# Module boundaries of a hybrid conformer and DeltaNet trunk: scaled activations in two PSUM banks, three tiles begun, weight subtractions on VectorE

## The chip, the cores and the metric

The kernel runs on one core of a Trainium2 chip (trn2). The time is device microseconds of one execution of the whole program. A core has five engines, each with its own queue of instructions: PE (TensorE, matmuls), DVE (VectorE), ACT (ScalarE), POOL (GpSimd) and SP (SyncE, which here issues the loads). They meet by semaphores. SBUF is the core's working memory; PSUM is the memory that matmuls write to, in eight banks of 512 float32 columns on 128 partitions.

## What is computed

A decoder trunk of two layers on 512 tokens of 1024 channels, batch 1. Each layer is a SwiGLU feed-forward module (FFN), a mixer, and a second FFN; the mixer is a causal convolution module in layer 0 and a gated DeltaNet in layer 1. Every module's input is normalised and modulated, and its output is added to the trunk through a gate:

```python
mod = (cs @ w_ada[i] + b_ada[i]).reshape(B, N_SUB, 3, D)
def modulated(x, j):
    shift, scale = mod[:, j, 0][:, None, :], mod[:, j, 1][:, None, :]
    return rms_norm(x, norm_g[i, j]) * (1.0 + scale) + shift
def gate(j):
    return 1.0 + mod[:, j, 2][:, None, :]
h = modulated(x, 0)
x = x + FFN_RES_WEIGHT * gate(0) * swiglu_ffn(h, w_ffn_in[i, 0], w_ffn_out[i, 0])
h = modulated(x, 1)
x = x + gate(1) * y          # y: conv_module(h) or gated_deltanet(h)
h = modulated(x, 2)
x = x + FFN_RES_WEIGHT * gate(2) * swiglu_ffn(h, w_ffn_in[i, 1], w_ffn_out[i, 1])
return rms_norm(x, final_g)  # after the last layer
```

## The kernel before

The trunk `x` lies in SBUF with channels on partitions, as eight blocks of 128 channels (k = 0 to 7) by 512 tokens. Float32 products are made of three matmuls: each operand is split into a high half, rounded to the matmul's type, and a low half, the remainder, and `mm3` adds high × high, low × high and high × low (L173, L174, L175) into one PSUM bank. A weight block comes by DMA as `raw`; ACT casts it to `whi` and DVE (L164, L165) or, at the boundaries, POOL (L206, L207) subtracts to get `wlo`. Activations likewise have `hh` and `hl`. Four buffers hold split weights, three hold raw ones.

In the FFNs `Feed` loads and splits weights ahead of the block that uses them: `block` prepares one more (`prep`) and takes the oldest ready one (`take`). In the FFNs of the first layer DVE also computes the modulation, by row sums `ajunk` over `w_ada` (L417), a few for each block (`ada_step`), with the rest in `ada_drain` ahead of `tail`.

Inside a module PE is fed densely. Where one module ends and the next begins stands `tail` (L210), at six places. It makes the last two blocks of output channels (6 and 7) in two halves of 256 tokens. For each half come the residual on DVE (`res`, L236), the square on ACT (L392), the sum over blocks on DVE (`ssum`, L397), the sum over channels on PE (`root`, L373, written to `aux`), the square root on ACT (L244), the reciprocal on DVE (L250) and the spread of the result over all partitions on PE (`bcast`, L368). Then `run` goes through k: `scaled` makes `t` on DVE (L260) and `hh` on ACT (L262), `low` makes `hl` on DVE (L272), and `head_k` issues the matmuls of the next module's first tiles. How many tiles are begun is in `EN`, by (layer, module). While half 0 runs, hooks at chosen k (`EH`) place half 1's residual, accumulation, root and spread, and one more weight split on POOL.

The region runs under a fixed order, so each engine executes as written here. Where only two tiles are begun, the third is made by 512-wide matmuls, of which some are filled in behind the second half's k. For `t` there are two buffers in SBUF. The last tail normalises for the output and has no next module.

The five that begin a module are, by time: FFN to convolution (near 390 us), convolution to FFN (600), FFN to the next layer's FFN (970), FFN to DeltaNet (1340), DeltaNet to FFN (1730).

Of the kernel before, what the change touches and what calls it, by code (L numbers as in the profile page):

```python
# [15 lines left out]
P = 128  # L16
T = 512
H2 = T // 2
D = 1024
KT = D // P  # L20
# [22 lines left out]
ENG={mybir.EngineType.PE,mybir.EngineType.Activation,mybir.EngineType.DVE,mybir.EngineType.Pool,mybir.EngineType.SP}  # L43
# [5 lines left out]
ARB = 3  # L49
# [10 lines left out]
ER = 7  # L60
EH = [1,2,3,3,5,6]
FH = [3,4,5,6]
MPL = [(),()]
EN = {(0,1):2,(0,2):2,(1,0):2,(1,1):3,(1,2):2}
LOP = [4,5,17,18,19,20,21,22,23,24]
IW = 3
IQ = [2,2,3,3]
# [40 lines left out]
def trunk_kernel(ctx: ExitStack, tc: tile.TileContext, x_in, c_in, vecs, consts, w_ada, w_st,  # L108
                 w_fi, w_fo, w_glu, w_tz, w_pw, w_dn, w_do, out):
    nc = tc.nc  # L110
    pe, act, dve, pool = nc.tensor, nc.scalar, nc.vector, nc.gpsimd

    keep = ctx.enter_context(tc.tile_pool(name="keep", bufs=1))
    wp = ctx.enter_context(tc.tile_pool(name="wp", bufs=4))
# [15 lines left out]
    def scratch(tag, shape=(P, T), dt=F32, bufs=1):  # L130
        return sc.tile(list(shape), dt, tag=tag, name=nm(tag), bufs=bufs)
# [22 lines left out]
    def load_raw(src, nk):  # L154
        raw = wp.tile([P, KT, P], F32, tag="raw", name=nm("raw"), bufs=3)
        with tc.high_priority(offset=WPRI):
            nc.sync.dma_start(raw[:, :nk, :], src)
        return raw

    def split_w(raw, nk):  # L160
        whi = wp.tile([P, KT, P], F32R, tag="whi", name=nm("whi"))
        wlo = wp.tile([P, KT, P], F32R, tag="wlo", name=nm("wlo"))
        with tc.high_priority(offset=WPRI):
            act.copy(whi[:, :nk, :], raw[:, :nk, :])  # L164
            dve.tensor_tensor(wlo[:, :nk, :], raw[:, :nk, :], whi[:, :nk, :].bitcast(F32), ALU.subtract)  # L165
        return whi, wlo

    def load_w(src, nk):
        return split_w(load_raw(src, nk), nk)
# [30 lines left out]

    edge = {}

    def split_pool(raw):
        whi = wp.tile([P, KT, P], F32R, tag="whi", name=nm("whi"))
        wlo = wp.tile([P, KT, P], F32R, tag="wlo", name=nm("wlo"))
        act.copy(whi, raw)  # L206
        pool.tensor_tensor(wlo, raw, whi.bitcast(F32), ALU.subtract)  # L207
        return whi, wlo

    def tail(src, nkt, mhi, mlo, layer, sub, norm, nxt, feed=None):  # L210
        nlayer, nsub, srcs = nxt or (0, 0, [])
        ms = (KT - 2, KT - 1)
        ps = {(m, i): mm_tile()[:, :H2] for m in ms for i in range(2)}
        if feed:
            feed.prep()
            ws = {m: feed.take() for m in ms}
            hw = feed.ready + [split_w(*r) for r in feed.raws]
        else:
            ws = {m: load_w(src(m, 0, KT), KT) for m in ms}
            hw = [load_w(s, KT) for s in srcs[:2]]  # L220
        raws = [load_raw(s, KT) for s in srcs[2:]]
        preload(AF.Sqrt, x[:, KT - 3, :1])
        region = ExitStack()
        region.enter_context(tc.manual_schedule(engines=ENG))

        sts = {}

        def mms(m, i, ks):
            sl = halves[i]
            for k in ks:  # L230
                mm3(ps[m, i], ws[m], k, mhi[:, k, sl], mlo[:, k, sl], k == 0, k == KT - 1)

        def res(m, i):
            j = (layer * 3 + sub) * KT + m
            sl = halves[i]
            dve.scalar_tensor_tensor(x[:, m, sl], ps[m, i], gate[:, j:j + 1], x[:, m, sl], ALU.mult, ALU.add)  # L236
            sts["sq"] = norm.square(x[:, m, sl], sl)
            return sts["sq"]

        def root(i):  # L240
            st = sts[i]
            pt = aux_tile()
            col_sum(pt, norm.t[:, halves[i]], 0)
            act.activation(st, pt[:, :2], AF.Sqrt, bias=eps, scale=1.0 / D)  # L244

        for i in range(2):
            sts[i] = scratch("rst", (P, 2), bufs=2)

        def inv_root(i):
            dve.reciprocal(sts[i], sts[i])  # L250

        def bcast(i):
            return spread([sts[i][:, g:g + 1] for g in range(2)])

        tv, hv = {}, {}

        def scaled(pb, k, i):
            j = (nlayer * 3 + nsub) * KT + k
            tv[k] = t = scratch("t", bufs=2)[:, :H2]
            dve.scalar_tensor_tensor(t, x[:, k, halves[i]], gain[:, j:j + 1], pb[:, :H2], ALU.mult, ALU.mult)  # L260
            shift = mod[:, nlayer, nsub * 24 + k:nsub * 24 + k + 1]
            act.activation(hh[:, k, halves[i]], t, AF.Identity, bias=shift)  # L262
            if k in MPL[i]:
                hv[k] = scratch("sil", bufs=2)[:, :H2]
                act.activation(hv[k], t, AF.Identity, bias=shift)

        def low(k, i):
            sl = halves[i]
            if k in MPL[i]:
                pool.tensor_tensor(hl[:, k, sl], hv[k], hh[:, k, sl].bitcast(F32), ALU.subtract)  # L270
                return
            dve.scalar_tensor_tensor(hl[:, k, sl], tv[k], mod[:, nlayer, nsub * 24 + k:nsub * 24 + k + 1],  # L272
                                     hh[:, k, sl].bitcast(F32), ALU.add, ALU.subtract)

        def head_k(i, k):
            sl = halves[i]
            for m, p in enumerate(hp):
                w = hw[m] if m < 2 else more[m - 2]
                mm3(p[:, sl], w, k, hh[:, k, sl], hl[:, k, sl], k == 0, k == KT - 1)

        def run(i, pb, hooks):
            for k in range(KT):
                scaled(pb, k, i)
                if k:
                    low(k - 1, i)
                    head_k(i, k - 1)
                for f in hooks.get(k, ()):
                    f()
            low(KT - 1, i)
            head_k(i, KT - 1)  # L290

        def final(i, pb, hooks):
            sl = halves[i]
            for k in range(KT):
                hooks.get(k, lambda: None)()
                dve.scalar_tensor_tensor(x[:, k, sl], x[:, k, sl], V("final_g", k), pb[:, :H2], ALU.mult, ALU.mult)
                if k % 2:
                    (nc.scalar if i and k % 4 == 3 else nc.sync).dma_start(out[i, :, k - 1:k + 1, :], x[:, k - 1:k + 1, sl])

        every = range(KT)  # L300
        mms(ms[0], 0, every)
        sq = res(ms[0], 0)
        mms(ms[1], 0, every)
        norm.accum(sq, halves[0])
        sq = res(ms[1], 0)
        norm.accum(sq, halves[0])
        mms(ms[0], 1, range(ER))
        root(0)
        inv_root(0)
        mms(ms[0], 1, range(ER, KT))  # L310
        more = [split_pool(raws[0])] if raws else []
        sq = res(ms[0], 1)
        mms(ms[1], 1, range(EK))
        pb = bcast(0)
        mms(ms[1], 1, range(EK, KT))
        if nxt is None:
            norm.accum(sq, halves[1])
            final(0, pb, {FH[0]: lambda: res(ms[1], 1), FH[1]: lambda: norm.accum(sts["sq"], halves[1]),
                          FH[2]: lambda: root(1), FH[3]: lambda: inv_root(1)})
            final(1, bcast(1), {})  # L320
            region.close()
            return
        box = {}
        hp = [mm_tile() for _ in range(EN[nlayer, nsub])]

        def late_res():
            box["sq"] = res(ms[1], 1)

        def late_root():
            root(1)  # L330

        def late_bcast():
            box["pb"] = bcast(1)

        hooks = {0: [lambda: norm.accum(sq, halves[1])]}
        for k, f in zip(EH, (late_res, lambda: norm.accum(box["sq"], halves[1]),
                             lambda: more.append(split_pool(raws[1])), late_root, lambda: inv_root(1), late_bcast)):
            hooks.setdefault(k, []).append(f)
        run(0, pb, hooks)
        run(1, box["pb"], {})  # L340
        region.close()
        edge["ps"], edge["w"] = hp, hw + more
# [78 lines left out]

    def ada_step(n):
        for _ in range(n):
            if len(ada["fly"]) == ARB:
                ada_use()
            ada_load()

# [17 lines left out]
    ada = {"plan": [], "fly": []}  # L445
# [37 lines left out]
    def ffn(layer, which, nxt, first=None):  # L483
# [4 lines left out]
        with tc.tile_pool(name=nm("ffn"), bufs=1) as ap, ExitStack() as ax:  # L488
# [15 lines left out]
            region = ax.enter_context(ExitStack())  # L504
            region.enter_context(tc.manual_schedule(engines=ENG))
            box = {}

            def step(n):
                if pump:
# [1248 lines left out]
```

## Time and profile before

| what | value |
|---|---|
| runs of the kernel, us | 2110.41, 2110.07, 2097.76; median 2110.07 |
| profiled execution, us | 2109.84, of which the span of the trace is 2108.1 |
| mean granted clock of TensorE | 0.977 |
| busy time of PE, DVE, ACT, POOL, us | 2022.4, 1209.2, 769.5, 226.2 |
| weight subtractions on DVE (L165, 128x1024 and 128x896) | 296, 361.6 us in all |
| weight subtractions on POOL (L207) | 11, mean 2404 ns |
| `t` (L260), `hh` (L262), `hl` (L272), mean of 80 each, ns | 478, 507, 629 |

A row of the timeline has the start, the length, the engine, the line and operation, output and inputs by name, and in brackets how long the engine was idle just before and what ended that. A row of the windows view has the stretch, its length, the busy time and count of PE, weight loads, DVE, ACT and POOL, the granted clock (1.00 is full), the DMA engines' share and GB/s. A row of PE's waits has the total in us, how often, and the longest. The lines of these views that matter stand in the prediction.

### The profile page before, as it was taken

To read this page: it belongs to the slowest core of one execution; us is meant where nothing else is said; L and a number is where in the kernel's file an instruction comes from. 1 tells how busy PE (TensorE), PEld (TensorE's weight loads), DVE (VectorE), ACT (ScalarE), POOL (GpSimd) and SP (SyncE) were. 2 spreads that over 40 slices of the span, in tenths; PEclk is the share of its full clock that TensorE was granted. 3 is DMA by queue.
4 is the path that set the end of the run, shared out by engine and by line. 5 is a ranking of instruction groups with operands and counts; after the bars stand their busy time and mean duration, and the time that the engine had idled before them with its cause. 6 is when DMAs were issued, how large, how long until landed. Compare 5 with 4: busy or idle time off the path is not lost.

```text
span 2108.1 us, 26022 instructions
## 1 busy us (share of the span) xinstructions
PE 2022.4 (96%) x10258; PEld 1683.7 (80%) x10258; DVE 1209.2 (57%) x1819; ACT 769.5 (37%) x1316; POOL 226.2 (11%) x150
## 2 busy tenths in 40 slices
PE   6999999898899999999999999989899999999998
PEld 4888888787888888888888888877677788888887
DVE  7666666799865655536333333777945574333334
ACT  5422222375542222224222222565345643222222
POOL 0000000289200000000000000125310100000000
PEclk9999999899899999999999999999989999999999
DMA  7667766222235656432333333322211132333332
GB/s 279 213 223 234 228 230 229 95 80 90 60 111 187 202 196 210 154 100 80 87 104 97 95 99 92 112 74 64 64 57 31 41 120 79 92 99 92 98 100 70
DMA packets 78332, 262.04 MB, mean 124 GB/s; under 512 B 8321, under 2 KB 14081, under 8 KB 78082
## 3 DMA queue, kind: packets, MB, share of 16 engines
q1 hardware_dynamic: 77666, 259.87, 38.6%
q8 instruction: 80, 1.31, 0.3%
q10 hardware_dynamic: 544, 0.52, 0.1%
q14 instruction: 42, 0.34, 0.1%
HBM read 254.59 MB, written 5.77 MB: 124 GB/s over the span
## 4 chain that ended last, share of the span: by engine, by line
PE 84%; DVE 8%; POOL 3%; ACT 2%; issue 2%; DMA 0%; POOLq 0%; DVEq 0%; SPq 0%; ACTq 0%
PE mm L173 26%; PE mm L174 25%; PE mm L175 25%; POOL pacc L661 3%; DVE t L1090 1%; PE mm L1415 1%; DVE hl L272 1%; DVE x L1166 1%; DVE x L1161 1%; PE mm L1437 1%; PE mm L1423 1%; PE mm L1642 1%; PE mm L1643 1%; PE aux L368 1%; PE mm L1646 1%
## 5 line engine op out<-in xcount | busy, mean ns | idle before, releaser
L174 PE MATMUL mm<-hl,whi 128*128 128x512 f32 (+1 forms) x1944 | 737.3, 380 | 17.2 <-DVE hl L272 16.6
L173 PE MATMUL mm<-hh,whi 128*128 128x512 f32 (+1 forms) x1944 | 742.6, 384 | 1.8 <-ACT hh L884 1.8
L175 PE MATMUL mm<-hh,wlo 128*128 128x512 f32 (+1 forms) x1944 | 734.7, 379 | 1.8 <-DVE wlo L165 1.8
L165 DVE TENSOR_TENSOR wlo<-raw,whi 128x1024 fp32r<-128x1024 f32 (+1 forms) x296 | 361.6, 1223 | 305.2 <-ACT whi L164 303.5
L174 PEld LDWEIGHTS mm<-hl,whi 128*128 128x128 f32 x1944 | 371.1, 191 | 87.0 <-DVE hl L272 22.0
L175 PEld LDWEIGHTS mm<-hh,wlo 128*128 128x128 f32 x1944 | 370.9, 191 | 71.5 <-DVE wlo L165 2.6
L173 PEld LDWEIGHTS mm<-hh,whi 128*128 128x128 f32 x1944 | 370.0, 191 | 71.5 <-issue 4.8
L164 ACT CAST whi<-raw 128x1024 fp32r<-128x1024 f32 (+1 forms) x296 | 301.7, 1023 | 247.3 <-PE mm L174 228.0
L173 PE MATMUL mm<-ahi,whi 128*128 128x512 f32 (+1 forms) x768 | 289.7, 377 | 0.0
L175 PE MATMUL mm<-ahi,wlo 128*128 128x512 f32 (+1 forms) x768 | 287.5, 374 | 0.0
L174 PE MATMUL mm<-alo,whi 128*128 128x512 f32 (+1 forms) x768 | 285.2, 371 | 0.0
L530 ACT CAST ahi<-t 128x512 fp32r<-128x512 f32 x88 | 54.7, 622 | 378.7 <-DVE t L526 378.7
L175 PEld LDWEIGHTS mm<-ahi,wlo 128*128 128x128 f32 x768 | 145.1, 189 | 28.2
L174 PEld LDWEIGHTS mm<-alo,whi 128*128 128x128 f32 x768 | 145.2, 189 | 27.0
L522 ACT ACTIVATE sil<-mm 128x512 f32<-128x512 f32 x88 | 52.7, 598 | 307.5 <-PE mm L175 303.8
L173 PEld LDWEIGHTS mm<-ahi,whi 128*128 128x128 f32 x768 | 145.4, 189 | 24.2
L207 POOL TENSOR_TENSOR wlo<-raw,whi 128x1024 fp32r<-128x1024 f32 x11 | 26.4, 2404 | 1226.6 <-ACT whi L206 1226.6
L417 DVE CUSTOM_DVE_ANT_0 ajunk<-araw,cs 128x1024 bf16<-128x1024 f32 x128 | 156.1, 1220 | 0.7
L526 DVE TENSOR_TENSOR t<-sil,mm 128x512 f32<-128x512 f32 x88 | 60.5, 688 | 157.8 <-PE mm L175 148.3
L461 DVE SCALAR_TENSOR_TENSOR x<-mm,gate,x 128x512 f32<-128x512 f32 x64 | 48.1, 751 | 143.5 <-PE mm L175 143.5
L531 DVE TENSOR_TENSOR alo<-t,ahi 128x512 fp32r<-128x512 f32 x88 | 60.9, 693 | 60.8 <-ACT ahi L530 60.8
L661 POOL TENSOR_TENSOR pacc<-pacc,pr 128x492 f32<-128x492 f32 (+11 forms) x58 | 83.3, 1437 | 18.6 <-ACT pr L660 14.5
(259 smaller groups left out, 1719.5 us busy)
## 6 DMA issues: line engine op xcount, KB each, us to landing
raw<-in_w_fi_dram SPq DMA_DIRECT2D x169, 512.0 KB, 3.5
araw<-in_w_ada_dram SPq DMA_DIRECT2D x128, 512.0 KB, 4.5
raw<-in_w_fo_dram SPq DMA_DIRECT2D x64, 448.0 KB, 3.3
raw<-in_w_dn_dram SPq DMA_DIRECT2D x33, 512.0 KB, 3.6
raw<-in_w_fo_dram SPq DMA_DIRECT2D x32, 512.0 KB, 3.5
stage<-in_w_ada_dram SPq DMA_DIRECT2D x16, 512.0 KB, 6.3
raw<-in_w_glu_dram SPq DMA_DIRECT2D x16, 512.0 KB, 3.5
raw<-in_w_pw_dram SPq DMA_DIRECT2D x8, 512.0 KB, 3.7
```

Of the source, the lines that this page charges most:

```text
L164: act.copy(whi[:, :nk, :], raw[:, :nk, :])
L165: dve.tensor_tensor(wlo[:, :nk, :], raw[:, :nk, :], whi[:, :nk, :].bitcast(F32), ALU.subtract)
L173: pe.matmul(ps, whi[:, k, :], mhi, start=first, stop=False)
L174: pe.matmul(ps, whi[:, k, :], mlo, start=False, stop=False)
L175: pe.matmul(ps, wlo[:, k, :], mhi, start=False, stop=last)
L417: dve.tensor_tensor_reduce(junk, raw, ada["cs"], 1.0, 0.0, ALU.mult, ALU.add, accum_out=mod[:, layer, col:col + 1])
L461: dve.scalar_tensor_tensor(x[:, m, sl], ps, gate[:, j:j + 1], x[:, m, sl], ALU.mult, ALU.add)
L522: act.activation(s, g, AF.Silu)
L526: dve.tensor_tensor(pr, box["s"], u, ALU.mult)
L530: act.copy(ahi[:, jj, :], pr)
L531: dve.tensor_tensor(alo[:, jj, :], pr, ahi[:, jj, :].bitcast(F32), ALU.subtract)
L661: pool.tensor_tensor(pacc[m][:, c], pacc[m][:, c], pr[:, c], ALU.add)
```

## The change

Scaled activations: `t` no longer comes from the SBUF scratch but from two PSUM banks, taken in turn by k. `EN` becomes 3 at three boundaries; the convolution's stays 2, the DeltaNet's was 3. Of the next module's four weights, the first is ready; the second's `whi` is cast by ACT ahead of the square root's table load, and its `wlo` is subtracted by DVE between the two accumulations of half 0; the third's `whi` and `wlo` follow the first residual of half 1, on ACT and DVE; only the fourth's `wlo` stays on POOL. `tail` no longer prepares or splits two weights ahead of its first residual. Each FFN prepares two more weights at its start, so that its feed runs one block further ahead. `ada_step` goes on using up loaded rows when nothing is left to load. `MPL` was empty and goes.

```diff
-MPL = [(),()]
-EN = {(0,1):2,(0,2):2,(1,0):2,(1,1):3,(1,2):2}
+EN = {(0,1):2,(0,2):3,(1,0):3,(1,1):3,(1,2):3}
...
+    def high(raw):
+        whi = wp.tile([P, KT, P], F32R, tag="whi", name=nm("whi"))
+        act.copy(whi, raw)
+        return whi
+
+    def rest(raw, whi, eng):
+        wlo = wp.tile([P, KT, P], F32R, tag="wlo", name=nm("wlo"))
+        eng.tensor_tensor(wlo, raw, whi.bitcast(F32), ALU.subtract)
+        return whi, wlo
...
+        region = ExitStack()
         if feed:
-            feed.prep()
             ws = {m: feed.take() for m in ms}
-            hw = feed.ready + [split_w(*r) for r in feed.raws]
+            hw = feed.ready
+            raws = [r for r, _ in feed.raws] + [load_raw(s, KT) for s in srcs[2:]]
+            region.enter_context(tc.manual_schedule(engines=ENG))
         else:
             ws = {m: load_w(src(m, 0, KT), KT) for m in ms}
-            hw = [load_w(s, KT) for s in srcs[:2]]
-        raws = [load_raw(s, KT) for s in srcs[2:]]
+            hw = [load_w(srcs[0], KT)]
+            raws = [load_raw(s, KT) for s in srcs[1:]]
+            region.enter_context(tc.manual_schedule(engines=ENG))
+        if raws:
+            hi1 = high(raws[0])
         preload(AF.Sqrt, x[:, KT - 3, :1])
...
-            tv[k] = t = scratch("t", bufs=2)[:, :H2]
+            tv[k] = t = box["t"][k % 2][:, :H2]
...
         norm.accum(sq, halves[0])
+        if raws:
+            hw.append(rest(raws[0], hi1, dve))
         sq = res(ms[1], 0)
         norm.accum(sq, halves[0])
         mms(ms[0], 1, range(ER))
         root(0)
         inv_root(0)
         mms(ms[0], 1, range(ER, KT))
-        more = [split_pool(raws[0])] if raws else []
         sq = res(ms[0], 1)
+        more = [rest(raws[1], high(raws[1]), dve)] if raws else []
...
         hp = [mm_tile() for _ in range(EN[nlayer, nsub])]
+        box["t"] = [mm_tile() for _ in range(2)]
...
-                             lambda: more.append(split_pool(raws[1])), late_root, lambda: inv_root(1), late_bcast)):
+                             lambda: more.append(split_pool(raws[2])), late_root, lambda: inv_root(1), late_bcast)):
...
-            if len(ada["fly"]) == ARB:
+            if len(ada["fly"]) == ARB or not ada["plan"] and ada["fly"]:
...
+            for _ in range(2):
+                feed.prep()
```

DVE's order at the boundary near 970 us, before. `mm` are the PSUM tiles of the last two output blocks, `ssum` the sum of squares:

```order
L165 TENSOR_TENSOR wlo_7245<-raw_7135,whi_7244 128x1024
L165 TENSOR_TENSOR wlo_7249<-raw_7170,whi_7248 128x1024
L236 SCALAR_TENSOR_TENSOR x<-mm_7240,gate,x 128x256
L397 TENSOR_TENSOR ssum_7059<-ssum_7059,sq_7287 128x256
L236 SCALAR_TENSOR_TENSOR x<-mm_7242,gate,x 128x256
L397 TENSOR_TENSOR ssum_7059<-ssum_7059,sq_7315 128x256
L250 RECIPROCAL rst_7260<-rst_7260 128x2
L236 SCALAR_TENSOR_TENSOR x<-mm_7241,gate,x 128x256
L260 SCALAR_TENSOR_TENSOR t_7383<-x,gain,aux_7360 128x256
L397 TENSOR_TENSOR ssum_7059<-ssum_7059,sq_7352 128x256
L260 SCALAR_TENSOR_TENSOR t_7387<-x,gain,aux_7360 128x256
L272 SCALAR_TENSOR_TENSOR hl<-t_7383,mod,hh 128x256
```

The same place after the change (L248 is the residual, L405 the accumulation, L209 the subtraction, L272 now `t` and L277 `hl`):

```order
L248 SCALAR_TENSOR_TENSOR x<-mm_7240,gate,x 128x256
L405 TENSOR_TENSOR ssum_7067<-ssum_7067,sq_7281 128x256
L209 TENSOR_TENSOR wlo_7308<-raw_7143,whi_7250 128x1024
L248 SCALAR_TENSOR_TENSOR x<-mm_7242,gate,x 128x256
L405 TENSOR_TENSOR ssum_7067<-ssum_7067,sq_7311 128x256
L262 RECIPROCAL rst_7254<-rst_7254 128x2
L248 SCALAR_TENSOR_TENSOR x<-mm_7241,gate,x 128x256
L209 TENSOR_TENSOR wlo_7348<-raw_7244,whi_7346 128x1024
L272 SCALAR_TENSOR_TENSOR mm_7380<-x,gain,aux_7356 128x256
L405 TENSOR_TENSOR ssum_7067<-ssum_7067,sq_7344 128x256
L272 SCALAR_TENSOR_TENSOR mm_7381<-x,gain,aux_7356 128x256
L277 SCALAR_TENSOR_TENSOR hl<-mm_7380,mod,hh 128x256
```

Two subtractions ahead of the first residual are gone; one stands between the accumulations and one ahead of the first `t`, which is written to a PSUM tile.

PE at the start of the next module near 600 us, before, for k = 0 and the start of k = 1, on tiles 4725 and 4726:

```order
L173 MATMUL mm_4725<-hh,whi_4586 128x256
L174 MATMUL mm_4725<-hl,whi_4586 128x256
L175 MATMUL mm_4725<-hh,wlo_4587 128x256
L173 MATMUL mm_4726<-hh,whi_4592 128x256
L174 MATMUL mm_4726<-hl,whi_4592 128x256
L175 MATMUL mm_4726<-hh,wlo_4593 128x256
L173 MATMUL mm_4725<-hh,whi_4586 128x256
```

And after the change (`mm3` is now at L172 to L174), on tiles 4711, 4712 and 4713:

```order
L172 MATMUL mm_4711<-hh,whi_4572 128x256
L173 MATMUL mm_4711<-hl,whi_4572 128x256
L174 MATMUL mm_4711<-hh,wlo_4573 128x256
L172 MATMUL mm_4712<-hh,whi_4584 128x256
L173 MATMUL mm_4712<-hl,whi_4584 128x256
L174 MATMUL mm_4712<-hh,wlo_4642 128x256
L172 MATMUL mm_4713<-hh,whi_4680 128x256
L173 MATMUL mm_4713<-hl,whi_4680 128x256
L174 MATMUL mm_4713<-hh,wlo_4682 128x256
L172 MATMUL mm_4711<-hh,whi_4572 128x256
```

Each k now has nine matmuls; the third weight's `wlo_4682` is first needed in the ninth matmul of k = 0.

More of the change, by code (lines that the diff above doesn't have):

```diff
@@ L213, in tail @@
         ps = {(m, i): mm_tile()[:, :H2] for m in ms for i in range(2)}
+        region = ExitStack()
         if feed:
-            feed.prep()
             ws = {m: feed.take() for m in ms}
-            hw = feed.ready + [split_w(*r) for r in feed.raws]
+            hw = feed.ready
+            raws = [r for r, _ in feed.raws] + [load_raw(s, KT) for s in srcs[2:]]
+            region.enter_context(tc.manual_schedule(engines=ENG))
         else:
             ws = {m: load_w(src(m, 0, KT), KT) for m in ms}
-            hw = [load_w(s, KT) for s in srcs[:2]]
-        raws = [load_raw(s, KT) for s in srcs[2:]]
+            hw = [load_w(srcs[0], KT)]
[3 more added lines that the diff above has]
+            hi1 = high(raws[0])
         preload(AF.Sqrt, x[:, KT - 3, :1])
-        region = ExitStack()
-        region.enter_context(tc.manual_schedule(engines=ENG))
         sts = {}
@@ L253, in bcast @@
             return spread([sts[i][:, g:g + 1] for g in range(2)])
-        tv, hv = {}, {}
+        tv = {}
         def scaled(pb, k, i):
             j = (nlayer * 3 + nsub) * KT + k
-            tv[k] = t = scratch("t", bufs=2)[:, :H2]
+            tv[k] = t = box["t"][k % 2][:, :H2]
             dve.scalar_tensor_tensor(t, x[:, k, halves[i]], gain[:, j:j + 1], pb[:, :H2], ALU.mult, ALU.mult)
[L261 to L265, printed above, removed]
+            act.activation(hh[:, k, halves[i]], t, AF.Identity, bias=mod[:, nlayer, nsub * 24 + k:nsub * 24 + k + 1])
         def low(k, i):
             sl = halves[i]
-            if k in MPL[i]:
-                pool.tensor_tensor(hl[:, k, sl], hv[k], hh[:, k, sl].bitcast(F32), ALU.subtract)
-                return
             dve.scalar_tensor_tensor(hl[:, k, sl], tv[k], mod[:, nlayer, nsub * 24 + k:nsub * 24 + k + 1],
```

## The prediction

> **What bounds the kernel now.** I read the page first, then the list of what PE (the matrix engine) waits for, then the six module boundaries on the timeline. The page's first line on the chain that ended last, its shares of the span by engine:
>
> ```profile
> PE 84%; DVE 8%; POOL 3%; ACT 2%; issue 2%; DMA 0%; POOLq 0%; DVEq 0%; SPq 0%; ACTq 0%
> ```
>
> The end is set by PE, and work on DVE cannot shorten it except where PE stands still. From PE's waits, the two that lie on lines this change touches (total us, times, longest):
>
> ```profile
> PE mm L174 <- DVE hl L272: 16.6, 17, 1.5
> PE aux L373 <- DVE ssum L397: 6.4, 3, 2.9
> ```
>
> So 23 us of idle PE wait for the low half `hl` and for the sum of squares. They lie at five boundaries, which I call B1 (FFN to convolution, near 390 us), B2 (600), B3 (970), B4 (1340) and B5 (1730). The timeline of PE has them one by one; the bracket is the idle time before the row.
>
> ```profile
> 389.94 1.01 PE L373 MATMUL aux<-ones,ssum 128*128 128x1 f32 x4 [2.85 <-DVE ssum L397]
> 403.20 0.39 PE L174 MATMUL mm<-hl,whi 128*128 128x256 f32 x1 [1.29 <-DVE hl L272]
> 405.47 0.38 PE L174 MATMUL mm<-hl,whi 128*128 128x256 f32 x1 [1.30 <-DVE hl L272]
> 407.98 0.39 PE L174 MATMUL mm<-hl,whi 128*128 128x256 f32 x1 [1.09 <-DVE hl L272]
> 410.24 0.58 PE L174 MATMUL mm<-hl,whi 128*128 128x256 f32 x1 [1.28 <-DVE hl L272]
> ...
> 602.96 0.39 PE L174 MATMUL mm<-hl,whi 128*128 128x256 f32 x1 [1.15 <-DVE hl L272]
> 609.08 0.39 PE L174 MATMUL mm<-hl,whi 128*128 128x256 f32 x1 [1.48 <-DVE hl L272]
> ...
> 967.37 0.61 PE L373 MATMUL aux<-ones,ssum 128*128 128x1 f32 x4 [1.98 <-DVE ssum L397]
> 973.07 0.39 PE L174 MATMUL mm<-hl,whi 128*128 128x256 f32 x1 [1.24 <-DVE hl L272]
> 979.23 0.38 PE L174 MATMUL mm<-hl,whi 128*128 128x256 f32 x1 [1.52 <-DVE hl L272]
> ...
> 1342.16 0.39 PE L174 MATMUL mm<-hl,whi 128*128 128x256 f32 x1 [1.23 <-DVE hl L272]
> 1348.34 0.39 PE L174 MATMUL mm<-hl,whi 128*128 128x256 f32 x1 [1.03 <-DVE hl L272]
> ...
> 1730.06 0.39 PE L174 MATMUL mm<-hl,whi 128*128 128x256 f32 x1 [1.23 <-DVE hl L272]
> 1736.18 0.39 PE L174 MATMUL mm<-hl,whi 128*128 128x256 f32 x1 [1.48 <-DVE hl L272]
> ```
>
> Some of the gaps cost twice, since the granted clock drops behind them. The windows view of four stretches (PE's busy time and PEclk are the columns to read):
>
> ```profile
> 389.32:396.15 6.83, 6.21 (x29) 6.21 (x30) 3.26 (x7) 2.56 (x6) 2.37 (x1) 0.50 0.21 69
> 409.80:416.63 6.83, 6.20 (x23) 5.41 (x24) 6.47 (x14) 3.55 (x7) 2.37 (x2) 0.50 0.12 49
> 979.83:983.24 3.41, 3.41 (x18) 3.38 (x17) 2.39 (x6) 1.17 (x3) 0.00 (x0) 0.50 0.42 154
> 1737.58:1741.00 3.42, 3.42 (x19) 3.42 (x18) 2.61 (x6) 1.41 (x3) 0.00 (x0) 0.50 0.35 140
> ```
>
> At half clock, half of each stretch is lost: 3.4, 3.4, 1.7 and 1.7 us. The drops follow gaps of 2.85, of four near 1.3, of 1.52 and of 1.48 us; the equal gap of 1.48 us in B2 was followed by none, so the drop is a matter of where the gap lies.
>
> Why `hl` is late shows on DVE and POOL (GpSimd) together, first in B2:
>
> ```profile
> 599.99 2.13 DVE L397 TENSOR_TENSOR ssum<-ssum,sq 128x256 f32<-128x256 f32 x1
> 605.25 0.48 DVE L260 SCALAR_TENSOR_TENSOR t<-x,gain,aux 128x256 f32<-128x256 f32 x1
> 606.16 0.48 DVE L260 SCALAR_TENSOR_TENSOR t<-x,gain,aux 128x256 f32<-128x256 f32 x1
> 607.20 1.83 DVE L272 SCALAR_TENSOR_TENSOR hl<-t,mod,hh 128x256 fp32r<-128x256 f32 x1 [0.56 <-ACT hh L262]
> ...
> 606.38 2.37 POOL L207 TENSOR_TENSOR wlo<-raw,whi 128x1024 fp32r<-128x1024 f32 x1 [4.54 <-ACT whi L206]
> ```
>
> The `hl` that starts inside the POOL subtraction at 606.38 ends just behind it (609.03 against 608.75); the accumulation at 599.99 lies beside POOL's other one and takes 2.13 us, where the accumulation quoted further down takes 0.43. In B1 POOL is busy far longer, with the convolution's `tz`, and DVE's two kinds of instruction part there:
>
> ```profile
> 400.74 4.39 POOL L616 TENSOR_TENSOR tz<-w,cst 128x1152 f32<-128x1152 f32 x2 [2.99 <-DMA w<-in_w_tz_dram]
> ...
> 403.18 0.48 DVE L260 SCALAR_TENSOR_TENSOR t<-x,gain,aux 128x256 f32<-128x256 f32 x1
> 403.58 1.83 DVE L272 SCALAR_TENSOR_TENSOR hl<-t,mod,hh 128x256 fp32r<-128x256 f32 x1
> ```
>
> Both run beside `tz`. `t` has one input in SBUF and one (`aux`) in PSUM and takes its usual 0.48 us; `hl` has two in SBUF and is held. With `t` in PSUM, `hl` has the inputs that `t` has now, so I take it at 0.48 us.
>
> [...]
>
> **The change part by part.** *Scaled activations in PSUM.* It frees `hl` from POOL. The gaps that go are the four in B1 (1.29 + 1.30 + 1.09 + 1.28 = 4.96 us) and the second one in the others: 1.48, 1.52, 1.03, 1.48. No row has a 256-wide `t` written to PSUM; the nearest two, one writing PSUM and one SBUF, both with one PSUM input:
>
> ```profile
> L676 DVE SCALAR_TENSOR_TENSOR aux<-u,vec,aux 128x511 f32<-128x511 f32 x5 | 3.7, 748 | 0.0
> L1090 DVE SCALAR_TENSOR_TENSOR t<-mm,vec,t 128x511 f32<-128x511 f32 x24 | 17.9, 747 | 22.9 <-POOL t L1095 13.1 <-ACT t L1087 9.7
> ```
>
> 748 against 747 ns: I cost the move at nothing, bounded by 0 and 0.1 us for each step k. DVE's pace is 606.16 − 605.25 = 0.91 us per k. Three tiles take PE nine 256-wide matmuls, 9 × 0.118 = 1.07 us, so where three are begun even 0.1 us more is covered; in B1 with two (0.71 us) PE waits for DVE, and 16 steps there would cost up to 1.6 us.
>
> [...]
>
> *Three tiles instead of two at B2, B3 and B5.* The third tile's 24 matmuls of 512 columns become 48 of 256. First and last starts of two runs of equal matmuls:
>
> ```profile
> 963.81 0.28 PE L173 MATMUL mm<-ahi,whi 128*128 128x256 f32 x1
> ...
> 965.11 0.28 PE L175 MATMUL mm<-ahi,wlo 128*128 128x256 f32 x1
> ...
> 699.69 0.39 PE L173 MATMUL mm<-ahi,whi 128*128 128x512 f32 x1
> ...
> 701.75 0.39 PE L173 MATMUL mm<-ahi,whi 128*128 128x512 f32 x1
> ```
>
> Eleven steps in 1.30 us are 0.118 each, nine in 2.06 are 0.229. 48 × 0.118 − 24 × 0.229 = 0.2 us more at each of three boundaries. In exchange PE's work per k exceeds DVE's pace.
>
> *Weight subtractions on DVE.* The second weight's is put between the two accumulations of half 0, the third's ahead of the first `t`. A pair of them, the split of a weight on ACT, and B2's rows round the first place:
>
> ```profile
> 384.80 2.36 DVE L165 TENSOR_TENSOR wlo<-raw,whi 128x1024 fp32r<-128x1024 f32 x2
> ...
> 598.32 1.05 ACT L206 CAST whi<-raw 128x1024 fp32r<-128x1024 f32 x1
> ...
> 595.12 0.49 DVE L236 SCALAR_TENSOR_TENSOR x<-mm,gate,x 128x256 f32<-128x256 f32 x1 [1.42 <-PE mm L175]
> 596.15 0.43 DVE L397 TENSOR_TENSOR ssum<-ssum,sq 128x256 f32<-128x256 f32 x1 [0.55 <-ACT sq L392]
> ...
> 597.44 0.50 PE L373 MATMUL aux<-ones,ssum 128*128 128x1 f32 x4
> ```
>
> One takes 1.18 us. DVE idles 1.42 us for PE just there, so it is hidden, with 0.24 us to spare and another 597.44 − 596.58 = 0.86 us before PE's column sum needs the result. Behind it are queued the second residual, its square and the accumulation.
>
> In B1 the pair at 384.80 stood ahead of the first residual and goes; one subtraction comes back between the sums: 2.85 − 2.36 + 1.18 = 1.67 us stay, 1.2 are won. In B3 the pair goes too, and the last `ada` reductions are taken earlier (the changed pump), so all 1.98 us go.
>
> The third weight's subtraction is the dear one. By B2's rows: residual at 598.43 on DVE, square on ACT to 599.3, the split to 600.35, subtraction to 601.55, then `t` 0.45, `hh` 0.5: 602.6, while PE is out of work at 602.96 − 1.15 = 601.81. That is 0.8 us, and `hl` 0.5 us later another 0.4 to 0.5: 1.3 us at each boundary, where today the first gap is 1.15 to 1.24. So the stall at the head of the next module is not removed; its cause moves from POOL to the chain ACT, DVE, ACT.
>
> *Feed one block further ahead.* A weight's split then waits for the buffer of the block just ending, while ACT's next instruction waits for that block as well; hidden. Uncovered, the price is 1.05 us of ACT per block.
>
> **The sum**, with gaps as quoted and 1.3 us of new head stall:
> - B1: 1.2 + 4.96 + half clock 6.8 lost of which I keep 1.0 (the 1.67 us gap may still cause a drop) = 5.8, less 1.3, less 1.0 for PE now waiting at DVE's pace: 9.7.
> - B2: 1.15 + 1.48 − 1.3 − 0.2 = 1.1.
> - B3: 1.98 + 1.24 + 1.52 + 1.7 − 1.3 − 0.2 = 4.9.
> - B4: 1.23 + 1.03 − 1.3 = 1.0.
> - B5: 1.23 + 1.48 + 1.7 − 1.3 − 0.2 = 2.9.
> - A matmul behind a gap takes 0.39 instead of 0.28 us; nine gaps fewer: 0.9.
>
> Together 20.5 us. The profiled execution took 2109.84 us (span 2108.1, 1.74 around it), within 0.3 us of the median 2110.07, so the forecast is 2109.84 − 20.5 = 2089.3 us, 1.0% less. The best that these rows allow is all gaps and half clocks gone, 2.85 + 4.96 + 6.8 in B1 and 2.6, 6.4, 2.3, 4.4 in the others: 30 us, about 2079; short waits beside them could add a few us.
>
> **The rivals.**
> - *The clock still drops.* Gaps of 1.3 us with smaller ones behind them are near those that brought a drop, and B2 shows that position decides. B1 keeps 5.8 us more, B3 and B5 1.7 each: 9.2 less, 2098.5. Against it: the four gaps in a row at 403 to 410 are surely apart now. Chance 0.2.
> - *PSUM does not free `hl`*, because its other input `hh` is in SBUF. The 403.18 row, with `x` in SBUF, speaks against it. Back come 4.96 and 3.4 in B1, less the 1.0 counted for pace, 1.48, 3.2, 1.03 and 3.2 in the others, and 0.8 of restarts: 17.1, so 2106.4. Chance 0.12.
> - *The column sum becomes the wait, and the kernel slower.* If the subtraction between the sums delays the second accumulation by over 0.86 us, as when ACT's extra split ahead of the table load delays the first square, PE stands before L373 at B2 to B5 as it does in B1 today: 2.85 and 3.4 of half clock each, 25.0, and B1 keeps its 1.2 and 2.4 more of half clock: 28.6, so 2117.9. The 0.24 + 0.86 us of room against one split of 1.05 speak against it, just. Chance 0.07.
> - *PE waits less than I count*, the head stall being filled and no clock lost: 2079. Chance 0.1.
>
> **How the numbers follow.** The forecast's own case has 0.51. It is as likely above as below 2089, the line of 1%, which is about what a measurement of this kernel can tell from no change. Half of it, the better case and a little of the clock's case make faster 0.41; the other half, the clock's rest, the unfreed `hl` and some of the column sum's case, which lies 0.4% above, make the same 0.55; slower 0.04. The range from 2076 (the better case with short waits) to 2107 (the unfreed `hl`) leaves out the slower case and a tail below.
>
> **What would show it.** Right: `hl` 0.5 us at most, no wait of PE for it over 0.6 us once a boundary's first k is past; PE's wait for the column sum at B1 alone, near 1.7 us; full clock at 410, 980 and 1738; a wait of 0.8 us for the first `hh` and 0.5 for the first `hl` at B2 to B5. Wrong: `hl` of 1.5 us or more while `tz` runs, waits before the column sum at B2 to B5, or waits of PE for a weight in the FFNs.

## The result and the profile after

Four runs of the changed kernel took 2077.81 to 2082.37 us, median 2078.69, beside a median of 2110.24 of the kernel before: a ratio of 0.9873, 95% interval 0.9845 to 0.9901. A second set, with runs of the kernel before on the same chip, took 2076.71 to 2079.85, ratio 0.985 (0.9834 to 0.9866). So the change makes the kernel faster by 1 to 1.7%: a larger gain than the forecast of 2089.3 us, inside its range and near its lower end. The profiled execution took 2082.37 us (span 2080.6), 27.5 us less than the profiled one before, where 20.5 had been worked out.

In the changed kernel `mm3` is at L172 to L174, the column sum at L381, the accumulation at L405, `t` at L272, `hh` at L273, `hl` at L277, the square root at L256. PE's waits there, from the list of waits (total us, times, longest), and behind them the one line of the view of L277:

```profile
PE mm L172 <- ACT hh L273: 3.7, 4, 0.9
PE aux L639 <- POOL tz L626: 3.4, 1, 3.4
PE aux L381 <- DVE ssum L405: 3.3, 2, 1.7
PE mm L173 <- DVE hl L277: 1.3, 6, 0.2
```

```profile
L277 DVE SCALAR_TENSOR_TENSOR hl<-mm,mod,hh x80: 475/479/486, 394.7 to 1721.5; 128x256 fp32r<-128x256 f32 x80
```

The waits for `hl` have shrunk from 16.6 to 1.3 us, and no `hl` takes more than 486 ns, where the longest took 2339. The sum of squares is late at B1 (1.7 us) and at the output, no longer at B3. In place of the first gap at B2 to B5 stand four waits for `hh`. At B2, DVE and PE:

```profile
593.06 1.23 DVE L209 TENSOR_TENSOR wlo<-raw,whi 128x1024 fp32r<-128x1024 f32 x1 [1.48 <-ACT whi L204]
594.20 0.48 DVE L272 SCALAR_TENSOR_TENSOR mm<-x,gain,aux 128x256 f32<-128x256 f32 x1
...
595.25 0.38 PE L172 MATMUL mm<-hh,whi 128*128 128x256 f32 x1 [0.89 <-ACT hh L273]
595.85 0.38 PE L173 MATMUL mm<-hl,whi 128*128 128x256 f32 x1 [0.22 <-DVE hl L277]
```

The subtraction waits for ACT's cast, `t` stands behind the subtraction, and PE waits 0.89 us for `hh` and 0.22 for `hl`, 1.1 us in all against 1.3 in the forecast.

Where the 27.5 us came from is seen best between the five square roots of half 0 (L244 before, L256 after), which cut the span at B1 to B5 and at the output. The windows view with these as limits, before and after (first column the stretch, then its length, PE's busy time, and PEclk third from the end):

```profile
390.99:597.97 206.98, 186.63 (x1057) 164.07 (x1058) 175.25 (x260) 115.55 (x187) 124.26 (x88) 0.91 0.25 78
597.97:968.01 370.04, 365.09 (x1697) 304.38 (x1697) 205.97 (x289) 107.51 (x143) 4.76 (x2) 1.00 0.50 164
968.01:1337.11 369.10, 366.00 (x1697) 305.76 (x1697) 148.12 (x179) 107.53 (x143) 4.77 (x2) 1.00 0.32 94
1337.11:1725.02 387.91, 362.19 (x2457) 296.78 (x2457) 262.25 (x514) 202.80 (x517) 87.47 (x52) 0.95 0.22 67
1725.02:2094.18 369.16, 366.11 (x1697) 305.77 (x1697) 145.90 (x177) 105.63 (x141) 4.77 (x2) 1.00 0.29 87
```

```profile
389.60:590.63 201.03, 184.24 (x1057) 162.22 (x1058) 168.94 (x261) 114.97 (x187) 121.03 (x87) 0.92 0.26 82
590.63:956.07 365.44, 364.33 (x1721) 305.48 (x1721) 205.50 (x290) 107.09 (x144) 2.39 (x1) 1.00 0.52 165
956.07:1321.50 365.43, 364.29 (x1721) 305.44 (x1721) 147.44 (x180) 107.09 (x143) 2.39 (x1) 1.00 0.32 95
1321.50:1701.28 379.78, 356.17 (x2457) 292.36 (x2457) 260.77 (x515) 202.12 (x516) 85.02 (x51) 0.97 0.22 69
1701.28:2066.71 365.43, 364.29 (x1721) 305.45 (x1721) 145.19 (x178) 105.33 (x141) 2.39 (x1) 1.00 0.29 88
```

| stretch | before | after | gain | of the forecast's sum |
|---|---|---|---|---|
| start to B1 | 390.99 | 389.60 | 1.4 | 1.2 |
| B1 to B2, with the convolution | 206.98 | 201.03 | 5.9 | 8.9 |
| B2 to B3, an FFN | 370.04 | 365.44 | 4.6 | 3.3 |
| B3 to B4, an FFN | 369.10 | 365.43 | 3.7 | 3.1 |
| B4 to B5, with the DeltaNet | 387.91 | 379.78 | 8.1 | 1.1 |
| B5 to the output, an FFN | 369.16 | 365.43 | 3.7 | 3.0 |

(The forecast's terms are sorted by where they fall: a boundary's column sum before the root, its head behind it; 0.1 us of restart for each gap.) The three FFN stretches are now alike within 0.01 us and only 1.1 us longer than PE's busy time in them. The surplus over the forecast lies in the stretch with the DeltaNet, where the change touches only the head at B4.

### The profile page after: what moved, and what is told of

Read it like the earlier page. It is cut to its first block, busy times and chain, and to the rows that moved or that the text cites. A ratio compares the mean times of both kernels' runs of the same rounds, so it can differ in the third digit from the quotient of the medians.

```text
span 2080.6 us, 26152 instructions
## 1 busy us (share of the span) xinstructions
PE 2009.1 (97%) x10330; PEld 1677.3 (81%) x10330; DVE 1201.0 (58%) x1824; ACT 767.6 (37%) x1316; POOL 213.4 (10%) x145
## 4 chain that ended last, share of the span: by engine, by line
PE 85%; DVE 7%; POOL 3%; ACT 2%; issue 2%; DMA 0%; POOLq 0%; DVEq 0%; SPq 0%; ACTq 0%
PE mm L172 26%; PE mm L173 26%; PE mm L174 26%; POOL pacc L671 3%; DVE t L1100 1%; PE mm L1425 1%; DVE x L1176 1%; DVE x L1171 1%; PE mm L1447 1%; PE mm L1652 1%; PE mm L1653 1%; PE mm L1433 1%; PE mm L1656 1%; PE mm L1415 1%; PE aux L639 1%
## 5 line engine op out<-in xcount | busy, mean ns | idle before, releaser
L172 PE MATMUL mm<-hh,whi 128*128 128x512 f32 (+1 forms) x1968 | 744.9, 380 | 5.4 <-ACT hh L273 3.7
L174 PE MATMUL mm<-hh,wlo 128*128 128x512 f32 (+1 forms) x1968 | 736.7, 375 | 1.9 <-DVE wlo L164 1.9
L164 DVE TENSOR_TENSOR wlo<-raw,whi 128x1024 fp32r<-128x1024 f32 (+1 forms) x291 | 356.1, 1225 | 306.7 <-ACT whi L163 301.9
L172 PEld LDWEIGHTS mm<-hh,whi 128*128 128x128 f32 x1968 | 372.5, 190 | 74.2 <-ACT hh L273 4.5
L174 PEld LDWEIGHTS mm<-hh,wlo 128*128 128x128 f32 x1968 | 373.3, 190 | 69.7 <-DVE wlo L164 2.9
L163 ACT CAST whi<-raw 128x1024 fp32r<-128x1024 f32 (+1 forms) x291 | 297.2, 1023 | 285.4 <-PE mm L173 258.2
L172 PE MATMUL mm<-ahi,whi 128*128 128x512 f32 (+1 forms) x768 | 289.3, 377 | 0.0
L174 PE MATMUL mm<-ahi,wlo 128*128 128x512 f32 (+1 forms) x768 | 287.0, 374 | 0.0
L174 PEld LDWEIGHTS mm<-ahi,wlo 128*128 128x128 f32 x768 | 144.6, 188 | 28.2
L172 PEld LDWEIGHTS mm<-ahi,whi 128*128 128x128 f32 x768 | 145.0, 189 | 24.2
L216 POOL TENSOR_TENSOR wlo<-raw,whi 128x1024 fp32r<-128x1024 f32 x6 | 14.4, 2397 | 837.8 <-ACT whi L215 837.8
```

Of the source, the lines that this page charges most:

```text
L172: pe.matmul(ps, whi[:, k, :], mhi, start=first, stop=False)
L174: pe.matmul(ps, wlo[:, k, :], mhi, start=False, stop=last)
```

## The experiments

The theory: `hl` was held because both its inputs lay in SBUF while POOL read SBUF, and the rest of the gain is PE's clock. The rivals: the moved weight subtractions did it, or the third tile. The stretches named below are those between square roots. Each ratio is to runs of the kernel before on the same chip; medians of different sections can come from different chips.

**One part undone: `t` back in SBUF.**

```diff
-            tv[k] = t = box["t"][k % 2][:, :H2]
+            tv[k] = t = scratch("t", bufs=2)[:, :H2]
```

> The changed kernel with one part undone: the scaled activations go back to two SBUF buffers. If hl is held because both its inputs are in SBUF while POOL reads SBUF, hl takes up to about 2 us again while the convolution's tz and POOL's one remaining subtraction run, PE's four gaps of 1.1 to 1.3 us at B1 come back with a half-clock stretch (5 + 3.4 us), and one gap near 1 us each at B2 to B5: 8 to 14 us more than the changed kernel, 2087 to 2093 us. If the gain came from the moved weight subtractions and the third tile alone, hl stays at 0.48 us and the time within 2 us of 2079.

2089.03 us (2088.5 to 2091.32), ratio to before 0.9923 (0.9897 to 0.995). The view of `hl` in this kernel, then DVE, POOL and PE at B1:

```profile
L277 DVE SCALAR_TENSOR_TENSOR hl<-t,mod,hh x80: 477/480/2342, 393.0 to 1728.2; 128x256 fp32r<-128x256 f32 x80
```

```profile
399.35 2.07 DVE L277 SCALAR_TENSOR_TENSOR hl<-t,mod,hh 128x256 fp32r<-128x256 f32 x1
...
398.60 2.54 POOL L216 TENSOR_TENSOR wlo<-raw,whi 128x1024 fp32r<-128x1024 f32 x1
...
401.48 0.58 PE L173 MATMUL mm<-hl,whi 128*128 128x256 f32 x1 [1.53 <-DVE hl L277]
```

The hold is back with the operand alone, up to 2342 ns; this `hl` ends just behind POOL's subtraction, at 401.42 against 401.14. B1 has four gaps of 0.72 to 1.53 us and two stretches of half clock (256-wide matmuls start 0.21 us apart behind 401.86 and 408.65 us, and 0.12 at full clock), B2 to B5 one gap of 0.98 to 1.02 each, so an FFN stretch takes 1.1 us more. The theory's range was 2087 to 2093; the first rival is out for this part.

**That part alone, on the kernel before.**

```diff
-            tv[k] = t = scratch("t", bufs=2)[:, :H2]
+            tv[k] = t = box["t"][k % 2][:, :H2]
...
+        box["t"] = [mm_tile() for _ in range(2)]
```

> The kernel before with one part alone: the scaled activations in two PSUM banks. hl should stay at 0.5 us; the four gaps at B1 and the second gap at B2 to B5 go, the waits for the column sum (2.85, 1.98) and the first gaps of 1.2 us behind the held accumulation stay: 9 us of gaps and up to 7 of half clock less than before, near 2094 where the kernel before is at 2110. If the parts work only together, 3 us or less.

2083.85 us (2080.68 to 2086.87), ratio 0.988 (0.9865 to 0.9896): 25 us less than before, not 16. The waits in the trace are the expected ones:

```profile
PE mm L174 <- DVE hl L272: 6.8, 9, 1.2
PE aux L374 <- DVE ssum L398: 6.4, 3, 2.8
```

What is left of the first is the held accumulation's five gaps of 1.15 to 1.23 us and four small ones. The column sum waits as before. At B2 the two kinds of instruction now part beside the same POOL line:

```profile
588.02 2.39 POOL L207 TENSOR_TENSOR wlo<-raw,whi 128x1024 fp32r<-128x1024 f32 x1 [52.36 <-ACT whi L206]
...
588.56 2.14 DVE L398 TENSOR_TENSOR ssum<-ssum,sq 128x256 f32<-128x256 f32 x1
...
594.91 2.38 POOL L207 TENSOR_TENSOR wlo<-raw,whi 128x1024 fp32r<-128x1024 f32 x1 [4.50 <-ACT whi L206]
...
595.72 0.48 DVE L272 SCALAR_TENSOR_TENSOR hl<-mm,mod,hh 128x256 fp32r<-128x256 f32 x1 [0.51 <-ACT hh L262]
```

The accumulation, with both inputs in SBUF, is held beside the first subtraction; `hl`, with one in PSUM, takes 0.48 us in the middle of the second. So this one edit brings about four fifths of the whole gain on that chip (25.4 of 31.4 us), the clock's part included. That is not a share that adds up with others: with `t` back in SBUF the other parts still bring 0.8% of the 1.3 to 1.5%, and between B3 and B4 this edit brings 2.7 of 3.7 us (366.42 us against 369.10 and 365.43). The size was missed by the clock: by the clock's record this profile's half-clock stretches, without the one at the end, sum to 51.2 us against 92.2 before, and half of the difference is 20.5 us, where I had allowed 7.

**Two tiles again at B2, B3 and B5.**

```diff
-EN = {(0,1):2,(0,2):3,(1,0):3,(1,1):3,(1,2):3}
+EN = {(0,1):2,(0,2):2,(1,0):2,(1,1):3,(1,2):2}
```

> The changed kernel with two tiles begun at B2, B3 and B5 again. If freeing hl did the work, PE's 0.71 us per step falls below DVE's 0.91 and small waits of up to 0.2 us per step return at three boundaries, less 0.2 us for the 512-wide third tile: 0 to 4 us more, 2079 to 2083 us. If the third tile is the main cover, 6 us or more.

2083.77 us (2081.84 to 2089.86), ratio 0.9904 (0.9871 to 0.9936). The FFN stretch:

```profile
588.57:955.18 366.61, 365.01 (x1697) 304.32 (x1697) 205.50 (x290) 107.00 (x143) 2.38 (x1) 1.00 0.51 165
```

366.61 against 365.44, so the third tile is worth 1.2 us at each of three boundaries, 3.5 us; the time's median lies 0.8 us above what was expected, with the clock's spread in it. It is a part, not the main cover.

**The third weight's subtraction back on POOL, once for the time and once for a trace.**

```diff
-        more = [rest(raws[1], high(raws[1]), dve)] if raws else []
+        more = [rest(raws[1], high(raws[1]), pool)] if raws else []
```

> The changed kernel with the third weight's subtraction on POOL, in the same place of the order. If the head of the next module waits for the chain ACT, DVE, ACT, the wait of 0.9 us for the first hh goes at B2 to B5, and a held accumulation (2.1 us) puts a wait of 1.2 us for the first hl in its place: within 3 us of the changed kernel. If moving this subtraction to DVE was a main part of the gain, 5 us or more lost.

> The changed kernel with the third subtraction on POOL again, for its trace. Its time, some 4 us under the changed kernel's, should come from the waits of 0.9 us for the first hh at B2 to B5, gone because t no longer stands behind the subtraction on DVE, with no accumulation of 2 us in their place, because the accumulation starts ahead of POOL's subtraction. If the accumulation is held, its 2 us row is there and the time was won elsewhere.

Ratio 0.985 (0.9811 to 0.9889), three runs of 2072.14 to 2075.25 us; the run for the trace took 2073.19. That is some 4 us under the changed kernel, more than the 3 us of the first expectation. A fourth run took 7084.77 us and is left out: in its trace the matmuls themselves are slow (a 512-wide one of L172 has a mean of 1103 ns, in the changed kernel 396) at a granted clock of 1.00, and the cause is open. At B2, in the second trace:

```profile
587.84 0.42 DVE L405 TENSOR_TENSOR ssum<-ssum,sq 128x256 f32<-128x256 f32 x1
...
588.31 2.40 POOL L209 TENSOR_TENSOR wlo<-raw,whi 128x1024 fp32r<-128x1024 f32 x1 [53.70 <-ACT whi L204]
```

```profile
585.83:949.98 364.15, 363.90 (x1721) 305.35 (x1721) 204.51 (x289) 106.92 (x144) 4.79 (x2) 1.00 0.51 166
```

The accumulation gets through ahead of POOL, where the first expectation had it held, `t` no longer stands behind the subtraction, and PE's wait shrinks to one of 0.3 us for the weight. The stretch is 1.3 us shorter. With `t` in PSUM and the square ahead of the cast, putting this subtraction on DVE costs time; the rival that it is a source of the gain is refuted.

**The third weight's cast ahead of the square on ACT.**

```diff
+        if raws:
+            hi2 = high(raws[1])
         sq = res(ms[0], 1)
-        more = [rest(raws[1], high(raws[1]), dve)] if raws else []
+        more = [rest(raws[1], hi2, dve)] if raws else []
```

> The changed kernel with the cast of the third weight ahead of the square of the first residual of half 1 on ACT, instead of behind it. If that chain sets the first hh, t starts 0.4 to 0.9 us earlier, the four waits of 0.9 us for hh shrink to at most 0.5 us, or turn into waits for hl of up to 0.5 us: 1 to 3 us less, near 2077. If the cast waits for its weight buffer anyway, no change within 1 us.

2073.88 us (2073.43 to 2076.25), ratio 0.9854 (0.9821 to 0.9886). ACT at B2, and the stretch:

```profile
588.86 1.05 ACT L204 CAST whi<-raw 128x1024 fp32r<-128x1024 f32 x1
589.82 0.41 ACT L402 ACTIVATE sq<-x 128x256 f32<-128x256 f32 x1
...
591.60 0.47 ACT L273 ACTIVATE hh<-mm,mod 128x256 fp32r<-128x256 f32 x1 [1.38 <-DVE mm L272]
```

```profile
588.52:952.93 364.41, 364.19 (x1721) 305.44 (x1721) 205.50 (x290) 107.02 (x143) 2.38 (x1) 1.00 0.51 166
```

In this kernel PE waits for no `hh` at B2 to B5 any more, and each FFN stretch is 1.0 us shorter, 0.2 above PE's busy time. The chain ACT, DVE, ACT was the wait, and the order on ACT its dear part. With the same at B4, where the waits are the same, four times 1.0 us is 4 of the 4.8 us between the medians, somewhat more than the 1 to 3 us expected.

**The second weight's subtraction moved too, and the changed kernel beside it.** The first edit is the one above; this is the second:

```diff
-        if raws:
-            hw.append(rest(raws[0], hi1, dve))
         sq = res(ms[1], 0)
         norm.accum(sq, halves[0])
+        if raws:
+            hw.append(rest(raws[0], hi1, dve))
```

> The changed kernel with the third weight's cast ahead of the square, and also the second weight's subtraction moved behind the second accumulation of half 0. At B1 the column sum's wait of 1.7 us should fall to about 0.5, and with it the half-clock stretch there; elsewhere DVE idles 1.7 us for the reciprocal at that place, so nothing is added: 5 to 8 us less than the changed kernel. If the reciprocal is late instead, PE waits for it before the spread at five boundaries and the time is not under that of the cast moved alone (4 to 5 us less).

> The changed kernel itself, on the same chip as the next three. If its time is a fixed part and half the length of its half-clock stretches, every run lies at one net time (about 2047 us) plus what its mean granted clock says was lost, and the stretches of this profile lie on another grid than those of the first. If the placement of instructions alone set the stretches, they lie where they lay.

On one chip the changed kernel took 2077.78 us, ratio 0.985 (0.9834 to 0.9866), and this one 2070.38 us (2068.88 to 2073.07), ratio 0.9818 (0.9803 to 0.9833): the fastest of all that were run, and 7.4 us under the changed kernel, as expected. Not all of it need be the edits': of the 9.2 us between the two profiles 2.5 lie in the stretch with the DeltaNet (379.42 against 376.88), where the cast accounts for about 1. The changed kernel's two profiles differ in the place of the clock's grid, by 0.36 us, and have net times (span less half of the half-clock stretches) of 2045.6 and 2044.5 us, 2 us under the expectation's. Of its column sums those at B1 and at the output wait, as the list of waits has it:

```profile
PE aux L383 <- DVE ssum L407: 2.1, 2, 1.5
PE mm L173 <- DVE hl L277: 1.3, 6, 0.2
```

2.1 − 1.5 leaves 0.6 us at B1, where it was 1.7, and the granted clock from B1's root to B2's is 0.94, where it was 0.92 and 0.93 in the changed kernel's two profiles. DVE's idle time ahead of the reciprocal (1.46 to 1.69 us at B2 to B5 in the changed kernel) covers the subtraction (1.23 us): PE's wait for the reciprocal is 0.6 us, once, in both kernels.

**The feed as deep as before.**

```diff
+            feed.prep()
             ws = {m: feed.take() for m in ms}
...
-            for _ in range(2):
+            for _ in range(0 if first else 1):
                 feed.prep()
```

> The changed kernel with the feed's depth as before: no (first FFN) or one (others) weight more prepared at an FFN's start instead of two, and the last one prepared at the boundary again. If the deeper feed is hidden, the net time is within 1 us of 2045 at B2 to B5; if the split ahead of a boundary's first residual matters, the column sum waits up to 1 us at some boundary and the time is 1 to 4 us over the changed kernel's.

2082.24 us (2077.14 to 2082.92), ratio 0.9907 (0.9874 to 0.994). The column sum at B1 waits as long as in the kernel before, and the FFN stretches from B2 and from B3 take 0.5 us more:

```profile
388.83 0.61 PE L382 MATMUL aux<-ones,ssum 128*128 128x1 f32 x4 [2.85 <-DVE ssum L406]
```

```profile
586.66:952.55 365.89, 364.57 (x1721) 305.58 (x1721) 204.02 (x290) 106.82 (x144) 2.39 (x1) 1.00 0.51 165
```

So the deeper feed takes a subtraction out of the boundary, and PE's waits show no price for it. Its net time is 2049.0 us, 3.4 and 4.5 over the changed kernel's two. Found are 0.5 us in each of the two stretches and, by the two kernels whose root at B1 starts earliest, some 1.2 us up to B1: it starts at 389.47 us here and at 388.26 and 388.12 in those (`t` in SBUF, and the third subtraction on POOL). Whether the rest of the 4 us between the medians is its work stays open, since the clock differs too.

**The row sums left to the drain.**

```diff
-            if len(ada["fly"]) == ARB or not ada["plan"] and ada["fly"]:
+            if len(ada["fly"]) == ARB:
```

> The changed kernel with the last row sums of the first layer left to the drain ahead of B3. If these made the column sum late at B3, its wait there returns with 0.8 us or more; if the two subtractions that stood there did, nothing changes.

2078.32 us, one run. At B3 the column sum waits again:

```profile
953.13 0.60 PE L381 MATMUL aux<-ones,ssum 128*128 128x1 f32 x4 [0.84 <-DVE ssum L405]
```

0.84 of the former 1.98 us is theirs; the other 1.1 is left, by subtraction, for the moved subtractions, which no run took alone.

**The kernel before, two more draws of the clock.**

> The kernel before itself, for another profile. If its own spread of 12 us is the clock's, its net time (span less half of the half-clock stretches) is again 2059 us, the grid of the stretches is shifted, and the difference in time is the difference in those stretches, most of it in the DeltaNet.

> The kernel before once more, for a third draw of the clock's grid: net time within 3 us of 2058 us, the half-clock stretches in the DeltaNet between 8 and 19 us of lost time, as in the two draws so far.

2102.52 and 2096.11 us. By the clock's record in the traces, the half-clock stretches of the three executions, with the one at the end, sum to 97.4, 89.1 and 78.9 us. Span less half of these: 2108.1 − 48.7 = 2059.4, 2100.8 − 44.5 = 2056.3, 2094.3 − 39.4 = 2054.9, within 4.5 us of each other where the spans differ by 13.8; the second and third lie some 3 us under what was expected of them. The stretch with the DeltaNet in the second and third execution of before, and in the second of the changed kernel:

```profile
1340.49:1718.92 378.43, 352.04 (x2457) 289.23 (x2457) 261.88 (x514) 202.54 (x516) 87.47 (x52) 0.98 0.22 69
```

```profile
1332.83:1712.45 379.62, 354.52 (x2457) 290.68 (x2457) 261.85 (x514) 202.72 (x516) 87.41 (x52) 0.97 0.22 69
```

```profile
1319.37:1698.79 379.42, 355.64 (x2457) 291.90 (x2457) 260.83 (x515) 201.96 (x517) 85.09 (x51) 0.97 0.22 69
```

387.91, 378.43 and 379.62 us of before against 379.78 and 379.42 of after: the 8.1 us that the two first profiles show for the DeltaNet are less than what the kernel before differs by from itself (9.5 us). But its first execution is no rare one. Of the 30 other runs of before on record 17 took 2107.9 to 2111 us, as it did, and those of them whose granted clock is on record had 0.976 or 0.977; no run of the changed kernel had less than 0.983. Whether the change makes the long stretches rarer, or they were not met by chance, is not shown. In the first execution of before two long stretches lay there:

```profile
1529.37:1536.20 6.83, 6.40 (x18) 4.84 (x19) 3.17 (x8) 4.79 (x8) 1.28 (x1) 0.50 0.00 2
1560.09:1573.74 13.65, 13.65 (x49) 10.67 (x48) 4.11 (x16) 1.64 (x6) 0.24 (x1) 0.50 0.00 0
```

They cost (6.83 + 13.65) / 2 = 10.2 us. At the same place of the program the other four executions have no counterpart to the long one, and to the other a single one half as long, in the third execution of before (1.7 us lost); the granted clock there was 0.80 from 1528 to 1580 us in the first execution of before, and 1.00 from 1511 to 1555 us in the first of the changed kernel.

## Why the prediction was right, and where its sizes were off

*What bounds.* Right: PE's gaps at the boundaries and the clock behind them. Undoing the operand alone brought the holds back. (Of the 23 us, 1.55 us stand at the output and not at the five boundaries; they stayed.)

*`t` in PSUM frees `hl`.* Right, at hardly any cost to DVE: the medians are 479 ns for `hl` against 480 before, and 490 for `t` against 481. The rival by which `hh` in SBUF would still hold it falls.

*The third tile.* The cost of 0.2 us did not show: with two tiles the FFN stretch is 1.2 us longer, and PE's busy time is 0.7 us of that (365.01 against 364.33). That the third tile covers DVE's pace was told but given no figure; against two tiles it is worth 1.2 us a boundary.

*Subtractions on DVE.* The column sum's 1.67 us at B1 came as 1.71; none waits at B2 to B5, so the slower rival falls. The new head stall was the term of the sum that was sized too high: 1.3 us each, measured 0.89 + 0.22 = 1.1 (the terms quoted for its first part end at 602.5, not 602.6), and at B1, where PE had run at half clock until 392.65, it did not show; in the kernel with `t` in SBUF B1 has it too, with 0.95 us for `hh`. Nor did the 1.0 us that I took for DVE's pace at B1: the waits for `hl` there are 0.4 us, and all six sum to 1.3. The smaller stall, the third tile's cost that did not show and a wait of 0.2 us for `hl` that the sum left out make up most of the 0.6 and 0.7 us by which the last two FFN stretches beat their sums; the first beat it by 1.3, with 0.8 us less of PE's busy time (365.09 to 364.33), about what three tiles save against two.

*The clock.* Of the 9.2 us counted for B1, B3 and B5, all came but 0.7 (B1 keeps one stretch, 1.7 us, where I kept 1.0). This is the clock's rival come true in small. The step that failed is the sum's silence on half clock elsewhere: it carries all of it over to the changed kernel, while the profiled execution of before lost 10.2 us in a part of the DeltaNet where the next two lost none and 1.7, and the changed kernel's two none. Of the 27.5 us, 7 come from there; the stretch with the convolution gave back some 3 in all, with longer waits for POOL's `tz` (from 1.7 to 3.4 us) and 1.7 us of half clock more. Against the medians, the forecast was 10.6 us too high, of which, by the two profiles, this is the larger part. That the changed kernel's mean clock is higher (0.983 to 0.985 in its eight runs, 0.976 to 0.983 in those of before) is measured; how much of it the five boundaries cause and how much the draw was not separated. That the time came out at the 2079 us of the last rival is luck: by that rival the head stall is filled and no clock is lost, and here the stall stood with 1.1 us and B1 kept a half-clock stretch.

## What to carry to other kernels

When an instruction takes far longer beside another engine's (here 2.07 us beside POOL instead of 0.48), look at where its inputs lie: with one of the two in PSUM instead of SBUF `hl` was no longer held, and this changed address alone brought 25 of the 31 us, though the other parts without it brought half or more. Price a small idle time of PE by the clock that follows it too (here 1.7 us lost behind a gap of 1.71 at B1), and take the profile of the kernel before more than once, since a single execution can hold 10 us of half clock that the next one of the same kernel does not. After such a change look again at the work that was moved to dodge the old conflict: it may now be cheaper where it was.

## What the runs showed of the hardware beyond that

In the first profiles of both kernels the half-clock stretches of one execution start on a common grid of 3.413 us: 409.80 − 389.32, 979.83 − 389.32 and 1737.58 − 389.32 us before are 6.0, 173.0 and 395.0 such steps, 1358.62 − 389.24 us after are 284.0. The grid's place differs from run to run, by up to about 1.4 us in the three profiles of before (starts at 389.32, 390.35 and 404.3 us, that is 0.2, 1.2 and 1.6 us into a step). In the changed kernel half clock followed a gap of 1.71 us at B1:

```profile
388.87 0.70 PE L381 MATMUL aux<-ones,ssum 128*128 128x1 f32 x4 [1.71 <-DVE ssum L405]
...
389.24:392.65 3.41, 3.41 (x18) 3.41 (x18) 0.88 (x3) 1.61 (x3) 0.00 (x0) 0.50 0.36 142
```

The length of the gap alone does not decide. That gap (387.16 to 388.87) lies inside one step of its grid, which runs from 385.83 to 389.24. The longer one of 2.85 us in the kernel with the feed undone (385.98 to 388.83) lies across an edge of its grid, at 387.65 (27 steps ahead of its half-clock stretch that starts at 479.80), with 1.67 us ahead of the edge, and the clock stays full:

```profile
386.00:400.00 14.00, 9.55 (x68) 8.44 (x69) 10.39 (x24) 6.26 (x14) 3.21 (x8) 1.00 0.38 128
```

An edge in the gap does not decide either: in the first profile of before the gap of 2.85 us at B1 (387.09 to 389.94) has one at 389.32, with 2.23 us ahead of it, and half clock starts at that edge. With `t` in PSUM alone, where the longest wait for the column sum is 2.8 us, the granted clock from B1's root to B2's is 0.94, as with the feed undone.

ACT's `hh` takes 475 ns with `t` in PSUM where it took 507 with `t` in SBUF, on average over 80 each, a gain of 32 ns that the prediction had not counted.
